# One more quartered pair in the up-projection, with one of the weights' sums made by an adding DMA

## The chip, the cores and the metric

One core of a Trainium2 chip runs the whole kernel. The metric is the device time of one execution in microseconds (us); of several runs the median counts. A profile of one further execution shows what each engine did: TensorE (PE, matmuls; its weight loads are PEld), VectorE (DVE), ScalarE (ACT), GpSimd (POOL), SyncE (SP, which here only issues DMAs) and the DMA engines.

## The reference

One decoder block on 512 tokens of width 1024, in float32: an attention sub-layer with two mixers, and a gated MLP with a short convolution. Only the second one's up-projection is touched:

```python
def conv_ffn(h, w_up, conv_w, conv_b, w_down):
    u = h @ w_up                       # (512, 1024) @ (1024, 2 * 2816)
    up = jnp.pad(u, ((0, 0), (CONV_WIDTH - 1, 0), (0, 0)))
    c = conv_b + conv_w[0] * up[:, 0:s]
    for j in range(1, CONV_WIDTH):
        c = c + conv_w[j] * up[:, j:j + s]
    val, gate = jnp.split(c, 2, axis=-1)
    return (jax.nn.silu(gate) * val) @ w_down
```

## The kernel before

Matmuls keep float32 accuracy by splitting each operand into a high part (rounded to the matmul's type, `whi`, made by ACT) and the low rest (`wlo`, made by DVE as raw − whi). A product is then three matmuls: high by high, high by low, low by high. `hh` and `hl` are the two parts of the normalized activations, features on the 128 partitions, tokens along the row.

The up-projection has 5632 output columns. They are worked off in 22 pairs: 128 gate columns and the 128 value columns that they will multiply. The list `order` says which columns come n-th; "pair 7" below is the pair at place 7 of `order`, counted from 0. A plain pair is two groups of 24 matmuls of 512 tokens (`dense_fm`), each into one PSUM bank. For places in `QUARTERED` the pair's product is computed in another way: the weights (1024 features by 256 columns) are cut in four quarters (upper or lower half of the features, gate or value columns: b11, b12 of the upper half, b21, b22 of the lower) and the tokens in halves. Sums of quarters by sums of the activations' quarters give the result with seven products in place of eight (Strassen's method in Winograd's form). Each product is 12 matmuls of 256 tokens, so a quartered pair is 84 matmuls of 256 in place of 48 of 512. The sums of the activations (`token_sums`) are made once, early; those of the weights for each pair, on DVE.

After each pair, `conv` takes gate and value out of PSUM (one ACT and two DVE instructions each, L129 and L141), Silu and the product with the value follow, and every second pair `sums` prepares sums and high and low parts for the down-projection, which uses the same trick.

The weights come through `wload`: SP issues a DMA into one of three places `raw` of 512 KB, which rotate. A plain pair needs two loads; a quartered pair two: "top" (upper half: b11 and b12) and "low" (b21, b22), each issued as two DMAs of 256 KB. Before, where the pair ahead was quartered too, "low" went to a fourth place, in the tile `right` (that was pair 8 alone). `first_quarters` makes what the first products need, ahead of the pair: the sums d, t1, t2 of the quarters, `h0`, `l0` (the parts of b11 and t1 for products −1 and 0) and `t3` (for product 2). `quartered` then makes `h1`, `l1` (t2 and b21) and `h2`, `l2` (the last ones) while PE is at the first products. Products 1 and 2 use the same bank `W` (tag `ps_a`), which ACT copies to `U` in `hB` between them.

Instructions are put in order per engine by a list scheduler when the program is built; each engine then works in that order and waits on semaphores.

The names in the rows: `ps_mm` and `ps_a` are the PSUM banks of results, `ps_b` a PSUM bank that here holds a weights' sum, `s` and `TS` the tiles with the activations' sums (and, in `s`, product 2's weights), `right` and `hB` the tiles in which pairs are finished. L1561 is the first matmul of a quartered pair, L126 the others, L123 those of plain pairs; L132 are tensor_tensor instructions of DVE, L323 the low parts of plain pairs' weights, L287 the loads of quartered pairs.

Of the kernel before, what the change touches and what calls it, by code (L numbers as in the profile page):

```python
# [16 lines left out]
ALU = mybir.AluOpType  # L17
# [7 lines left out]
KT = D // 128  # L25
# [58 lines left out]
def hybrid_block(ctx: ExitStack, tc: tile.TileContext, A: dict, out: bass.AP):  # L84
    nc = tc.nc
# [33 lines left out]
    def pb():  # L119
        return bank("b", 2)  # L120
# [10 lines left out]
    def tt(o, a, b, op):  # L131
        v.tensor_tensor(o, a, b, op=op)  # L132
# [7 lines left out]
    def stt(o, a, s, b, op0=ALU.mult, op1=ALU.add):  # L140
        v.scalar_tensor_tensor(o, a, s, b, op0=op0, op1=op1)  # L141
# [23 lines left out]
    for name in ("rwkv_mu", "rwkv_w0", "rwkv_a0", "rwkv_k_k", "rwkv_k_a", "rwkv_r_k", "rwkv_ln_g", "rwkv_ln_b"):  # L165
        r0, n = ROWS[name]
# [51 lines left out]
    hl = hp.tile([128, KT, S], F32R, name="hl", tag="hl")  # L218

    order = [f for i in range(NFH) for f in (i, NFH + i)]  # L220
    QUARTERED = (5, 7, 8, 10, 12, 14, 16, 18)

    def weight_tiles():
        def cols(w, o, kt=KT, eng=v):
            return w[:, o:o + 128], kt, 128, eng

        def rows(w, o, n, kt=KT, eng=v):
            step = 1024 // n
            for i, k0 in enumerate(range(0, kt, step)):
                kn = min(step, kt - k0)  # L230
                yield w[128 * k0:128 * (k0 + kn), o:o + n], kn, n, eng[i] if type(eng) is list else eng

        pool_ = nc.gpsimd
        yield cols(w_in, O_RWKV + 1536, eng=pool_)
        yield cols(w_in, O_RWKV + 1664, eng=pool_)
        for p in range(NH2):
            for o in (512, 0, 1024):
                yield cols(w_in, O_RWKV + o + 128 * p)
        yield cols(w_in, O_KC)
        yield from rows(w_in, O_Q, 512, eng=[v, pool_, ("spare", pool_), v])  # L240
        yield cols(w_in, O_VC)
        yield from rows(w_in, O_KS, 256, eng=[v, ("spare", v)])
        for m in range(NGA):
            yield cols(w_in, O_GA + 128 * m)
        yield from rows(w_in, O_KW, 280, eng=pool_)
        for m in range(NGA, KT):
            if m < 4:
                for s4 in range(m if m > NGA else 0, m + 1):
                    for s_ in "kv":
                        yield A["cmp_w1_" + s_][0][512 * s4:512 * s4 + 512], 4, 256, "ab" if (s4, s_) == (3, "k") else None  # L250
            yield cols(w_in, O_GA + 128 * m)
        for m in range(NGB):
            yield cols(w_in, O_GB + 128 * m)
        for m in range(KT):
            if m + NGB < KT:
                yield cols(w_in, O_GB + 128 * (m + NGB), eng=pool_ if m else v)
            yield cols(A["w_proj_b"][0], 128 * m, NH2, eng=pool_)
        for m in range(KT):
            yield cols(A["w_proj_a"][0], 128 * m, NH2)
        yield from rows(A["w_out"][0], 0, 512)  # L260
        yield from rows(A["w_out"][0], 512, 512, eng=())
        for n_, f in enumerate(order):
            if n_ in QUARTERED:
                for kh in range(2):
                    yield A["w_up"][0][512 * kh:512 * kh + 512], KT, 128, ("quarters", f, kh and n_ - 1 in QUARTERED)
            else:
                yield cols(A["w_up"][0], DFF + 128 * f)
                yield cols(A["w_up"][0], 128 * f)
# [3 lines left out]
    def wload():  # L272
        nxt = next(wtiles, None)
        if nxt is None:
            if spent:
                spent[0]()
        else:
            src, kt, n, eng = nxt
            if eng == "ab":
                raw, eng = AB[:, 0].rearrange("p a r t -> p (a r t)").rearrange("p (k n) -> p k n", n=n), None  # L280
            elif type(eng) is tuple and eng[:1] == ("quarters",) and eng[2]:
                raw = right[:, 6:8].rearrange("p a (k n) -> p (a k) n", n=n)
            else:
                raw = wp.tile([128, kt, n], F32, name="raw", tag=f"raw{next(slots) % 3}", bufs=1)
            if type(eng) is tuple and eng[:1] == ("quarters",):
                for i, c0 in enumerate((DFF + 128 * eng[1], 128 * eng[1])):
                    nc.sync.dma_start(raw[:, 4 * i:4 * i + 4], src[:, c0:c0 + 128].rearrange("(k p) n -> p k n", p=128))  # L287
                eng = "quarters"
            else:
                nc.sync.dma_start(raw, src.rearrange("(k p) n -> p k n", p=128))  # L290
            loads.append((raw, kt, n, eng))
# [64 lines left out]
    with tc.manual_schedule(engines={getattr(mybir.EngineType, e) for e in ("PE", "Activation", "DVE", "Pool")}):  # L356
# [3 lines left out]
        hi = wp.tile([128, KT, 128], F32R, name="whi", tag="whi", bufs=2)  # L360
        lo = wp.tile([128, KT, 128], F32R, name="wlo", tag="wlo", bufs=2)
        raw = loads.pop(0)[0]
# [21 lines left out]
        r0, n = ROWS["rwkv_mu"]  # L384
# [260 lines left out]
    for k in range(31):  # L645
        m, n = 31 - k, k + 1
# [845 lines left out]
    def token_sums():  # L1492
        for kh in range(2):
            def total(o, K, i):
                ks, ns = slice(4 * K + 2 * kh, 4 * K + 2 * kh + 2), slice(256 * i, 256 * i + 256)
                tt(o, hh[:, ks, ns].bitcast(F32), hl[:, ks, ns].bitcast(F32), ALU.add)

            x, y, z, w = [right[:, i].rearrange("p (k n) -> p k n", k=2) for i in range(3, 7)]
            total(x, 0, 1)
            total(y, 1, 1)  # L1500
            tt(y, x, y, ALU.add)
            yield
            total(z, 0, 0)
            tt(x, z, x, ALU.subtract)
            tt(z, y, z, ALU.subtract)
            yield
            total(w, 1, 0)
            tt(w, w, z, ALU.subtract)
            for j, o in enumerate((y, z, x, w)):
                hi, lo = sum_parts(j, kh)  # L1510
                act(hi, o)
                tt(lo, o, hi.bitcast(F32), ALU.subtract)
                if j % 2:
                    yield
# [9 lines left out]
    def halves(hi, lo, x):  # L1524
        act(hi, x)
        tt(lo, x, hi.bitcast(F32), ALU.subtract)
# [6 lines left out]
    def by_quarter(w):  # L1533
        return w.rearrange("p (q k) n -> p q k n", q=2)

    def first_quarters(top, low):
        b11, b12, b21, b22 = top[:, 0:4], top[:, 4:8], low[:, 0:4], low[:, 4:8]
        hi, lo = two_quarters()
        d = pb().rearrange("p (k n) -> p k n", k=4)
        tt(d, b22, b12, ALU.subtract)  # L1540
        tt(b12, b12, b11, ALU.subtract)
        halves(hi, lo, by_quarter(top))
        tt(b11, b22, b12, ALU.subtract)
        y = 2 * (next(turnsq) % 2)
        t3 = [split[y + j][:, :, NFH - 3].rearrange("p q (k n) -> p q k n", k=2) for j in range(2)]
        halves(*t3, by_quarter(d))
        return b11, low, (hi, lo), t3

    def quartered():
        t2, low, (h0, l0), (h3, l3) = ahead.pop(0)  # L1550
        b21 = low[:, 0:4]
        G, V, W = mmb(), mmb(), pa()[:, 0:256]
        act(V[:, 0:256], kc[:, 0:256], AF.Copy, scale=0.0)
        U = hB[:, 256 * (NFH + 3):256 * (NFH + 5)]

        def product(o, hi, lo, j, start=False):
            his, los = ([w[:, k] if len(w.shape) == 3 else w[:, k // 2, k % 2] for k in range(4)] for w in (hi, lo))
            for k in range(4):
                mh, ml = moving(j, k)
                if start and k == 0:  # L1560
                    te.matmul(o, lhsT=his[k], rhs=mh, start=True, stop=False, skip_group_check=True)  # L1561
                else:
                    mm_on(o, his[k], mh, False)
                mm_on(o, his[k], ml, False)
            for k in range(4):
                mm_on(o, los[k], moving(j, k)[0], False)

        wload()
        h1, l1 = two_quarters()
        halves(h1[:, 0], l1[:, 0], t2)  # L1570
        halves(h1[:, 1], l1[:, 1], b21)
        product(W, h0[:, 0], l0[:, 0], -1, True)
        act(G[:, 0:256], W)
        product(V[:, 0:256], h0[:, 1], l0[:, 1], 0)
        act(V[:, 256:512], V[:, 0:256])
        h2, l2 = two_quarters()
        tt(b21, b21, t2, ALU.subtract)
        halves(h2, l2, by_quarter(low))
        product(W, h1[:, 0], l1[:, 0], 1)
        act(U[:, 0:256], W)  # L1580
        product(G[:, 0:256], h1[:, 1], l1[:, 1], -2)
        wsplit()
        product(W, h3, l3, 2)
        act(G[:, 256:512], W)
        act(U[:, 256:512], W)
        product(V[:, 0:256], h2[:, 1], l2[:, 1], 3)
        product(G[:, 256:512], h2[:, 0], l2[:, 0], -3)
        tt(V, V, U, ALU.add)
        return G, V

    def sums(i, lf, rt):
# [257 lines left out]
```

## Time and profile before

| | |
|---|---|
| median of 3 runs | 806.47 us (805.72 to 807.74) |
| profiled execution | 805.58 us, its span 803.8 us |
| PE busy | 797.0 us (99%) |
| DVE busy | 634.9 us (79%) |
| ACT busy | 457.7 us (57%) |
| POOL busy | 64.7 us (8%) |
| first matmuls of the 8 quartered pairs | 515.4 to 652.1 us |
| granted TensorE clock | 0.999 of full speed |

The span runs from the first to the last instruction; the execution's own time has some overhead around it. A row of the timeline gives start, duration, engine, line, operation, out<-in with shapes, how many were merged, and in brackets how long the engine was idle before it and what ended that. A row of a windows table gives, for each engine, busy time and the number of instructions. The queues of SP and POOL are written SPq and POOLq where DMAs are issued.

### The profile page before, as it was taken

The numbers are of one execution on the slowest core, as the hardware profiler recorded it, in microseconds if no ns is written. First come the engines' busy times: TensorE is split into PE (matmuls) and PEld (weight loads), VectorE is DVE, ScalarE is ACT, GpSimd is POOL, SyncE is SP. The second block draws the span as 40 slices with busy tenths as digits, with TensorE's granted clock in tenths as the row PEclk, the third lists the DMA queues.
The fourth block names the chain that finished last, engine by engine and source line by source line (L and its number), as shares of the span: only waits on it lengthen the run. The fifth ranks groups of instructions, "written<-read, shape, count | busy, mean of one in ns | idle before, by whom it ended". The sixth has DMA issues, their size and how long they took to land.

```text
span 803.8 us, 14340 instructions
## 1 busy us (share of the span) xinstructions
PE 797.0 (99%) x5541; PEld 664.4 (83%) x5541; DVE 634.9 (79%) x1227; ACT 457.7 (57%) x931; POOL 64.7 (8%) x96
## 2 busy tenths in 40 slices
PE   8999999999999999999999999999999999999998
PEld 7777788987777887787788898899999998888886
DVE  6477869993665678889675589999999987898895
ACT  6766654563444568778334375666666665446452
POOL 6200011032000044011000000000000000000010
PEclk9999999999999999999999999999999999999999
DMA  8433213227562231001258322233233334376821
GB/s 240 115 79 79 79 54 105 70 81 208 143 117 68 70 83 50 15 27 32 63 177 283 103 83 82 83 108 115 86 103 106 105 106 129 120 235 220 276 95 52
DMA packets 114512, 89.30 MB, mean 111 GB/s; under 512 B 4886, under 2 KB 99021, under 8 KB 114189
## 3 DMA queue, kind: packets, MB, share of 16 engines
q1 hardware_dynamic: 110960, 82.83, 35.4%
q0 software_dynamic: 2432, 3.09, 1.5%
q10 hardware_dynamic: 1052, 2.48, 0.9%
q8 instruction: 43, 0.70, 0.4%
q14 instruction: 25, 0.20, 0.1%
HBM read 82.35 MB, written 4.39 MB: 108 GB/s over the span
## 4 chain that ended last, share of the span: by engine, by line
PE 94%; DVE 3%; ACT 1%; issue 0%; DMA 0%; DVEq 0%; ACTq 0%
PE ps_mm L123 62%; PE ps_mm L126 9%; PE ps_a L123 7%; PE ps_a L126 6%; PE ps_b L123 4%; PE ps_b L126 2%; PE ps_b L1304 1%; PE ps_mm L1304 1%; DVE P L1230 0%; DMA xt<-in_x_dram 0%; DVE P L136 0%; ACT P L129 0%; PE ps_b L591 0%; DVE wlo L132 0%; PE ps_b L560 0%
## 5 line engine op out<-in xcount | busy, mean ns | idle before, releaser
L123 PE MATMUL ps_mm<-hh,whi 128*128 128x512 f32 (+1 forms) x496 | 192.8, 391 | 0.3 <-DVE hl L141 0.3
L123 PE MATMUL ps_mm<-hl,whi 128*128 128x512 f32 (+1 forms) x496 | 190.6, 387 | 0.0
L129 ACT ACTIVATE whi<-raw 128x1024 fp32r<-128x1024 f32 (+2 forms) x132 | 124.5, 944 | 111.9 <-PE ps_mm L123 70.3
L123 PE MATMUL ps_mm<-hh,wlo 128*128 128x512 f32 (+1 forms) x496 | 120.4, 383 | 0.0
L323 DVE TENSOR_TENSOR wlo<-raw,whi 128x1024 fp32r<-128x1024 f32 (+1 forms) x73 | 84.7, 1162 | 41.7 <-PE ps_mm L123 21.6
L123 PEld LDWEIGHTS ps_mm<-hh,whi 128*128 128x128 f32 x496 | 93.2, 188 | 21.8 <-issue 1.3
L123 PEld LDWEIGHTS ps_mm<-hl,whi 128*128 128x128 f32 x496 | 93.3, 188 | 17.8 <-issue 1.0
L123 PEld LDWEIGHTS ps_mm<-hh,wlo 128*128 128x128 f32 x496 | 91.1, 188 | 18.5
L132 DVE TENSOR_TENSOR wlo<-raw,whi 128x1024 fp32r<-128x1024 f32 (+1 forms) x46 | 46.9, 1023 | 7.8 <-ACT whi L129 5.3
L141 DVE SCALAR_TENSOR_TENSOR right<-ps_mm,cw,right 128x511 f32<-128x511 f32 (+1 forms) x56 | 41.1, 743 | 4.4 <-ACT right L129 4.2
L129 ACT ACTIVATE P<-P,nm 128x512 f32<-128x512 f32 (+3 forms) x64 | 35.4, 554 | 11.4 <-DVE nm L1230 10.9
L323 POOL TENSOR_TENSOR wlo<-raw,whi 128x512 fp32r<-128x512 f32 (+3 forms) x13 | 20.9, 1605 | 177.0 <-PE ps_mm L123 142.6
L1746 POOL DMA_DIRECT2D out_dram<-XP x4 | 2.2, 549 | 391.3 <-DMA raw<-in_w_down_dram 389.7
L1230 DVE CUSTOM_DVE_ANT_0 P<-ps_a,AB 128x512 f32<-128x512 f32 (+3 forms) x64 | 29.3, 484 | 1.8 <-PE ps_a L123 1.5
L129 ACT ACTIVATE right<-ps_mm,cw 128x512 f32<-128x512 f32 x28 | 21.4, 772 | 9.9 <-DVE ps_mm L132 7.8
L129 ACT ACTIVATE QK<-ps_mm 128x64 f32<-128x64 f32 (+5 forms) x56 | 14.9, 308 | 18.0 <-PE ps_mm L123 17.9
L123 PE MATMUL ps_mm<-whi,hh 128*128 128x280 f32 (+2 forms) x72 | 22.4, 331 | 0.0
L123 PE MATMUL ps_mm<-whi,hl 128*128 128x280 f32 (+2 forms) x72 | 21.8, 323 | 0.0
L129 ACT ACTIVATE whi<-T 128x1024 fp32r<-128x1024 f32 (+1 forms) x12 | 11.9, 991 | 16.4 <-DVE T L132 7.5
L132 DVE TENSOR_TENSOR raw<-raw 128x512 f32<-128x512 f32 (+1 forms) x25 | 18.7, 747 | 2.7 <-DMA raw<-in_w_down_dram 2.7
L129 ACT ACTIVATE whi<-hA 128x1024 fp32r<-128x1024 f32 (+1 forms) x14 | 13.4, 969 | 12.8 <-PE ps_mm L126 3.7
L123 PE MATMUL ps_mm<-obT,whi 128*128 128x512 f32 x64 | 20.7, 399 | 0.0
(498 smaller groups left out, 1856.7 us busy)
## 6 DMA issues: line engine op xcount, KB each, us to landing
raw<-in_w_in_dram SPq DMA_DIRECT2D x38, 512.0 KB, 3.9
raw<-in_w_up_dram SPq DMA_DIRECT2D x28, 512.0 KB, 3.9
raw<-in_w_down_dram SPq DMA_DIRECT2D x18, 512.0 KB, 3.9
raw<-in_w_up_dram SPq DMA_DIRECT2D x30, 256.0 KB, 3.8
hA<-in_w_down_dram SPq DMA_DIRECT2D x12, 512.0 KB, 4.5
raw<-in_w_out_dram SPq DMA_DIRECT2D x8, 512.0 KB, 4.7
xt<-in_x_dram SPq DMA_DIRECT2D x4, 512.0 KB, 4.6
raw<-in_cmp_w_v_dram SPq DMA_DIRECT2D x4, 512.0 KB, 3.8
```

The lines of the kernel that those rows point to most:

```text
L123: te.matmul(o, lhsT=l, rhs=r, start=start, stop=stop)
L126: te.matmul(o, lhsT=l, rhs=r, start=False, stop=stop, skip_group_check=True)
L129: sc.activation(o, i, f, **kw)
L132: v.tensor_tensor(o, a, b, op=op)
L141: v.scalar_tensor_tensor(o, a, s, b, op0=op0, op1=op1)
L323: low = eng.tensor_tensor(lo, raw, hi.bitcast(F32), op=ALU.subtract)
L1230: maxima.append(v.tensor_tensor_reduce(out=P[:, i], in0=o, in1=BT[:, h, 384 - 128 * qt:512], scale=-1.0, scalar=-NEG, op0=ALU.add, op1=ALU ...
L1304: te.transpose(pt[:, 128 * i:128 * i + 128], P[:, 4 * x + i, 128 * k:128 * k + 128], ident)
L1746: queue.dma_start(out[0][128 * t:128 * t + 128, 512 * hf + cs.start:512 * hf + cs.stop], o)
```

## The change

Places 5, 7, 8, 10, 11, 13, 14, 16, 18 are quartered in place of 5, 7, 8, 10, 12, 14, 16, 18: nine pairs, and three times two in a row. The fourth raw place goes. The signs of some sums are moved from the weights to the activations, so that the first sum of the weights is an addition, b12 + b11, and that one is made by a DMA that adds: once "top" has landed, GpSimd issues a transfer from its one half to the other with `accum_op=add`. The value columns come out with the other sign, which the last combination takes back.

```diff
-    QUARTERED = (5, 7, 8, 10, 12, 14, 16, 18)
+    QUARTERED = (5, 7, 8, 10, 11, 13, 14, 16, 18)
...
-            elif type(eng) is tuple and eng[:1] == ("quarters",) and eng[2]:
-                raw = right[:, 6:8].rearrange("p a (k n) -> p (a k) n", n=n)
             else:
                 raw = wp.tile([128, kt, n], F32, name="raw", tag=f"raw{next(slots) % 3}", bufs=1)
             if type(eng) is tuple and eng[:1] == ("quarters",):
                 for i, c0 in enumerate((DFF + 128 * eng[1], 128 * eng[1])):
                     nc.sync.dma_start(raw[:, 4 * i:4 * i + 4], src[:, c0:c0 + 128].rearrange("(k p) n -> p k n", p=128))
+                if not eng[2]:
+                    nc.gpsimd.dma_start(raw[:, 4:8], raw[:, 0:4], accum_op=ALU.add)
...
     (token_sums)
-            tt(y, x, y, ALU.add)
+            tt(y, y, x, ALU.subtract)
...
-            tt(z, y, z, ALU.subtract)
+            stt(z, y, -1.0, z, ALU.mult, ALU.subtract)
...
-            tt(w, w, z, ALU.subtract)
+            stt(w, w, -1.0, z, ALU.mult, ALU.subtract)
...
     def first_quarters(top, low):
-        b11, b12, b21, b22 = top[:, 0:4], top[:, 4:8], low[:, 0:4], low[:, 4:8]
+        b11, t1, b22 = top[:, 0:4], top[:, 4:8], low[:, 4:8]
         hi, lo = two_quarters()
-        d = pb().rearrange("p (k n) -> p k n", k=4)
-        tt(d, b22, b12, ALU.subtract)
-        tt(b12, b12, b11, ALU.subtract)
         halves(hi, lo, by_quarter(top))
-        tt(b11, b22, b12, ALU.subtract)
+        t2 = pb().rearrange("p (k n) -> p k n", k=4)
+        tt(t2, b22, t1, ALU.add)
+        tt(b11, t2, b11, ALU.subtract)
...
-        halves(*t3, by_quarter(d))
-        return b11, low, (hi, lo), t3
+        halves(*t3, by_quarter(b11))
+        return t2, low, (hi, lo), t3
...
     (quartered)
-        tt(b21, b21, t2, ALU.subtract)
+        tt(b21, t2, b21, ALU.add)
...
-        tt(V, V, U, ALU.add)
+        stt(V, V, -1.0, U, ALU.mult, ALU.subtract)
```

How the instructions stand now. GpSimd's queue, from the attention part to the end of the program, after:

```order
L323 TENSOR_TENSOR wlo<-raw,whi 128x512 x7
L287 DMA raw<-raw 128x512 x9
L1745 DMA out_dram<-XP 128x512 x4
```

The nine adding transfers (L287 of the changed kernel) stand alone between the split of the attention part's last weights and the first stores.

SP's queue, the loads of pairs 5 to 15 (4 DMAs a quartered pair, 2 a plain one; `128x4x128` is a quarter, `128x8x128` half a plain pair), before and after:

```order
-L287 DMA raw<-in_w_up_dram 128x4x128 x4
-L287 DMA right<-in_w_up_dram 128x4x128
+L285 DMA raw<-in_w_up_dram 128x4x128 x4
 L290 DMA raw<-in_w_up_dram 128x8x128 x2
-L287 DMA raw<-in_w_up_dram 128x4x128 x6
+L285 DMA raw<-in_w_up_dram 128x4x128 x8
 L290 DMA raw<-in_w_up_dram 128x8x128 x2
-L287 DMA raw<-in_w_up_dram 128x4x128 x4
+L285 DMA raw<-in_w_up_dram 128x4x128 x8
 L290 DMA raw<-in_w_up_dram 128x8x128 x2
```

The loads into `right` are gone, and eight quarters stand in a row where two quartered pairs do.

DVE, the preparation of pair 7 while PE is at pair 6 (`ps_b<-raw` is the pair's first sum on DVE, d before and t2 after; `wlo` of 128x1024 is `l0`):

```order
 L132 TENSOR_TENSOR ps_b<-raw 128x512
 L141 SCALAR_TENSOR_TENSOR right<-ps_mm,cw,right 128x510
-L132 TENSOR_TENSOR raw<-raw 128x512
-L132 TENSOR_TENSOR s_5189<-ps_b,s_5188 128x2x256
+L132 TENSOR_TENSOR wlo<-raw,whi 128x1024
 L132 TENSOR_TENSOR right<-hB,right 128x512
 L141 SCALAR_TENSOR_TENSOR right<-ps_mm,cw,right 128x511
```

The sum on DVE is gone, product 2's part has moved back, and `l0` has moved to the front.

PE in pair 8, from the second half of product 1 (`ps_a<-TS,whi`) to the start of product 2 (`ps_a<-s_5188,s_5186`). Before:

```order
L126 MATMUL ps_a<-TS,whi 128x256 x4
L126 MATMUL ps_mm<-hh_4674,whi 128x256
L126 MATMUL ps_mm<-hl_4675,whi 128x256
L126 MATMUL ps_mm<-hh_4674,whi 128x256
L126 MATMUL ps_mm<-hl_4675,whi 128x256
L126 MATMUL ps_mm<-hh_4674,whi 128x256
L126 MATMUL ps_mm<-hl_4675,whi 128x256
L126 MATMUL ps_mm<-hh_4674,whi 128x256
L126 MATMUL ps_mm<-hl_4675,whi 128x256
L126 MATMUL ps_mm<-hh_4674,wlo 128x256 x3
L126 MATMUL ps_a<-s_5187,wlo 128x256 x2
L126 MATMUL ps_a<-TS,wlo 128x256 x2
L126 MATMUL ps_mm<-hh_4674,wlo 128x256
L126 MATMUL ps_a<-s_5188,s_5186 128x256 x4
```

After, the same pair:

```order
L126 MATMUL ps_a<-TS,whi 128x256 x4
L126 MATMUL ps_a<-s_5187,wlo 128x256 x2
L126 MATMUL ps_a<-TS,wlo 128x256 x2
L126 MATMUL ps_mm<-hh_4674,whi 128x256
L126 MATMUL ps_mm<-hl_4675,whi 128x256
L126 MATMUL ps_mm<-hh_4674,whi 128x256
L126 MATMUL ps_mm<-hl_4675,whi 128x256
L126 MATMUL ps_mm<-hh_4674,whi 128x256
L126 MATMUL ps_mm<-hl_4675,whi 128x256
L126 MATMUL ps_mm<-hh_4674,whi 128x256
L126 MATMUL ps_mm<-hl_4675,whi 128x256
L126 MATMUL ps_mm<-hh_4674,wlo 128x256 x4
L126 MATMUL ps_a<-s_5188,s_5186 128x256 x4
```

Product 1's low half (`ps_a<-s_5187,wlo`) stood in the midst of another product, one matmul ahead of product 2; now twelve matmuls stand between. In pair 14 of the changed kernel it stands so:

```order
L126 MATMUL ps_a<-s_5187,wlo 128x256 x2
L126 MATMUL ps_a<-TS,wlo 128x256 x2
L126 MATMUL ps_mm<-hh_4674,whi 128x256
L126 MATMUL ps_mm<-hl_4675,whi 128x256
L126 MATMUL ps_a<-s_5188,s_5186 128x256 x3
L126 MATMUL ps_mm<-hh_4674,wlo 128x256 x4
L126 MATMUL ps_a<-s_5188,s_5186 128x256
```

There two matmuls stand between product 1's end and product 2. In the other quartered pairs of the changed kernel it is twelve.

More of the change, by code (lines that the diff above doesn't have):

```diff
@@ L264, in weight_tiles @@
                 for kh in range(2):
-                    yield A["w_up"][0][512 * kh:512 * kh + 512], KT, 128, ("quarters", f, kh and n_ - 1 in QUARTERED)
+                    yield A["w_up"][0][512 * kh:512 * kh + 512], KT, 128, ("quarters", f, kh)
             else:
```

## The prediction

> **What bounds the kernel now.** I read the page's head and its chain of work first, then the busy times in stretches of the up-projection, then single rows there.
>
> ```profile
> span 803.8 us, 14340 instructions
> PE 797.0 (99%) x5541; PEld 664.4 (83%) x5541; DVE 634.9 (79%) x1227; ACT 457.7 (57%) x931; POOL 64.7 (8%) x96
> PE 94%; DVE 3%; ACT 1%; issue 0%; DMA 0%; DVEq 0%; ACTq 0%
> ```
>
> TensorE (PE) is busy for 99% of the span and carries 94% of the chain. A change moves the time only by removing matmul time or by making PE wait. The changed part runs from 515.4 us (the first quartered pair) to 662. The windows below are, in this order, pairs 7, 8, 9 together (two quartered, one plain), then twice one quartered and one plain pair (10 and 11; 12 and 13).
>
> ```profile
> core 0: us, PE busy (x) PEld busy (x) DVE busy (x) ACT busy (x) POOL busy (x), PEclk, DMA share, GB/s
> 536.50:568.17 31.67, 31.31 (x218) 29.21 (x216) 30.46 (x48) 20.99 (x39) 0.00 (x0) 1.00 0.29 84
> 568.17:589.15 20.98, 20.98 (x134) 19.08 (x132) 19.30 (x31) 13.12 (x24) 0.00 (x0) 1.00 0.35 101
> 589.15:610.13 20.98, 20.98 (x134) 19.09 (x132) 19.14 (x30) 12.84 (x25) 0.00 (x0) 1.00 0.35 101
> ```
>
> The granted clock is 1.00 throughout, GpSimd (POOL) is idle, the DMA engines are a third busy, and VectorE (DVE) is the second engine: 91% in the alternating stretch and 96% where two quartered pairs stand together (30.46 of 31.67).
>
> Prices of the two kinds of pair: a plain group of 24 matmuls, and a quartered pair from its first matmul (L1561) to the next pair's.
>
> ```profile
> 477.34 0.39 PE L123 MATMUL ps_mm<-hh,whi 128*128 128x512 f32 x1
> 482.78 0.39 PE L123 MATMUL ps_mm<-hh,whi 128*128 128x512 f32 x1
> ...
> 536.50 0.28 PE L1561 MATMUL ps_a<-hh,whi 128*128 128x256 f32 x1
> 546.57 0.28 PE L1561 MATMUL ps_a<-hh,whi 128*128 128x256 f32 x1
> ```
>
> A plain group takes 482.78 − 477.34 = 5.44 us, so a plain pair 10.88. A quartered pair takes 546.57 − 536.50 = 10.07; from the alternating window it is 20.98 − 10.88 = 10.10.
>
> **The change, part by part.**
>
> *The ninth quartered pair.* One plain pair becomes a quartered one: 48 matmuls of 512 columns leave, 84 of 256 come. 10.88 − 10.08 = 0.80 us less on PE, and PE is the bound. The ninth pair brings its own work beside it, on ACT and DVE (below).
>
> *The stall in pair 8.* The whole up-projection has one wait of PE:
>
> ```profile
> PE ps_a L126 <- ACT hB L129: 0.4, 1, 0.4
> ...
> 552.21 0.28 PE L126 MATMUL ps_mm<-hh,wlo 128*128 128x256 f32 x1
> 552.84 0.39 PE L126 MATMUL ps_a<-s,s 128*128 128x256 f32 x1 [0.36 <-ACT hB L129]
> ...
> 552.41 0.38 ACT L129 ACTIVATE hB<-ps_a 128x256 f32<-128x256 f32 x1 [1.86 <-PE ps_a L126]
> ```
>
> Product 2 reuses the bank of product 1, which ACT must first copy out (552.41, 0.38). One matmul of 0.12 us stands between them, because the order of before put product 1's low half behind the K half of another product. From 552.21 to 552.84 is 0.63 where 0.12 would do: 0.5 us lost (the window's 31.67 against 20.98 + 10.08 = 31.06 says 0.6; I take 0.6). The new order of pair 8 has twelve matmuls there, so this goes: −0.6. The same interleaving now stands in pair 14, with two matmuls between: 0.5 − 0.12, so +0.4.
>
> *VectorE.* Two stretches' difference prices a quartered pair on DVE: 30.46 − 19.2 = 11.3 us, a plain one 19.2 − 11.3 = 7.9.
>
> ```profile
> L132 DVE TENSOR_TENSOR raw<-raw 128x512 f32<-128x512 f32 x20 | 13.6, 682 | 0.0
> L132 DVE TENSOR_TENSOR ps_b<-raw 128x512 f32<-128x512 f32 x6 | 4.1, 689 | 0.0
> L323 DVE TENSOR_TENSOR wlo<-raw,whi 128x1024 fp32r<-128x1024 f32 x12 | 14.6, 1218 | 0.9 <-ACT whi L129 0.9
> 529.21 0.69 DVE L132 TENSOR_TENSOR ps_b<-raw 128x512 f32<-128x512 f32 x1
> 529.80 0.74 DVE L141 SCALAR_TENSOR_TENSOR right<-ps_mm,cw,right 128x510 f32<-128x510 f32 x1
> ...
> 534.92 1.22 DVE L132 TENSOR_TENSOR wlo<-raw,whi 128x1024 fp32r<-128x1024 f32 x1
> ```
>
> Of three sums (682 and 689 ns, starting 0.59 apart) one leaves DVE per pair: 10.7 us. Reading t2 from PSUM instead of SBUF, and the sums that become scalar_tensor_tensor (0.74 against 0.69), are 0.05 each: nothing. Two quartered pairs and a plain one then need 2 × 10.7 + 7.9 = 29.3 of PE's 31.06 us (94%; before 96%), but such groups come three times in a row, pairs 7 to 15, where before there was one. One and one need 18.6 of 20.98. Spare: 1.8 and 2.4 us per group. ACT does as many instructions per quartered pair as before (21 of 31.7 us busy): covered.
>
> *The waits that move with it.* The first pieces now come from the high half: h0's low part stood at 534.92, 5.7 us after the pair's first sum; in the new order it is the second instruction after it. t2, and what hangs on it, is needed on PE only at the second and third product (12 and 24 matmuls of 0.12, 1.4 and 2.9 us later). So the late load, low's, has more time than before. No fourth place: the top place is free once t2 is in PSUM, so low of 8, 11, 14 can go there; their loads start when the pair before has its first pieces (for pair 7 534.92 + 1.22 = 536.1, 10 us before pair 8's first matmul), against 3.8 us to land (next fence). Covered.
>
> *The adding transfer.* Per pair POOL issues one transfer of 256 KB that adds b11 to b12 on chip. The trace has none that adds. Nearest rows: on-chip transfers of the POOL queue (KH), and its 256 KB stores.
>
> ```profile
> L1073 POOL DMA_DIRECT2D KH<-KH x4: 509/512/576, 279.1 to 285.6; - x4
> DMA to landing us min/median/max: 2.2/2.5/3.9
> out_dram<-XP POOLq DMA_DIRECT2D x4, 256.0 KB, 2.8
> ...
> raw<-in_w_up_dram SPq DMA_DIRECT2D x30, 256.0 KB, 3.8
> 522.09 0.92 SPq L287 DMA_DIRECT2D raw<-in_w_up_dram  x2
> 552.33 0.92 SPq L287 DMA_DIRECT2D raw<-in_w_up_dram  x2
> 574.57 0.98 SPq L287 DMA_DIRECT2D raw<-in_w_up_dram  x2
> ...
> 562.07 0.69 DVE L132 TENSOR_TENSOR ps_b<-raw 128x512 f32<-128x512 f32 x1
> 581.86 0.69 DVE L132 TENSOR_TENSOR ps_b<-raw 128x512 f32<-128x512 f32 x1
> ```
>
> Bounds of issue to landing: 2.2 us (the fastest on-chip one), and 7.8 (the slowest, 3.9, twice, since an addition also reads its target). I take 3.5: the store of the same size, 2.8, and a quarter more. Issuing it costs POOL 0.51 us, and POOL has nothing else there: behind its waits queue only the next adding transfers and, 100 us later, the stores. Is it in time? On DVE the sum t2 waits for it, and all evictions queue behind t2. Pair 7: the second top load starts at about 522.5, lands 3.8 later at 526.3, the sum lands at 529.8; t2's turn is at 529.2. Pair 10: 552.8 + 3.8 + 3.5 = 560.1 against 562.07. Pairs like 12 of before (now 16, 18): 575.05 + 3.8 + 3.5 = 582.35 against 581.86. So DVE waits about half a microsecond at three pairs, under its spare 1.8 to 2.4: nothing on PE. Pairs 8, 11, 14 have their top loaded a pair ahead: covered. Below zero this edit can't go on PE beyond the 0.6 already counted, since PE waits nowhere else.
>
> The row: POOL issues took 0.51 us at 279 us beside a working DVE. [...]
>
> **The sum.** −0.8 − 0.6 + 0.4 = −1.0 us. The profiled execution took 805.58 us (span 803.8 and 1.8 around it), 0.9 below the runs' median of 806.47. The runs spread over 2.0 us, so about 0.3% (2.4 us) is what can be told from no change. For the median: 806.47 − 1.0 = 805.5.
>
> **Rivals.**
>
> A. *DVE becomes the bound in the second of two quartered pairs.* For it: the only stall of before sits in such a pair, with DVE at 96%. Against: one sum less per pair, and the alternating stretch shows no stall at 91%. If 8, 11 and 14 each lose 0.6, it is 1.8 in place of 0.4: 806.9.
>
> B. *The adding transfer is late; slower than before.* With L its time to landing, DVE stands idle for L − 2.9 at pair 7, L − 3.0 at 16 and 18, L − 5.5 at 10 and 13 (from the landings above), less the spare 1.8, 2.4 and 1.8. [...] At 7.8 it is 3.1 + 2 × 2.4 + 2 × 0.5 = 8.9: 814.4. It is slower by over 0.3% from L = 6.3 on (3L − 15.5 = 3.4). For it: no row shows an addition. Against: all POOL rows are at 3.9 or less, and an addition would have to double the slowest.
>
> C. *Pair 14 doesn't stall* since DVE is less loaded than the order's maker assumed: 805.1.
>
> D. *The ninth pair's gain doesn't show.* Half of it could be lost where the extra start-up of a pair is not hidden; then 805.9, not told from the forecast.
>
> **How the numbers follow.** Forecast with D 0.62, A 0.18, B 0.11 (two thirds of it beyond L = 6.3), C 0.07, something unseen 0.02. The largest gain, 0.8 + 0.6 = 1.4, is 0.17%, so faster by over 0.3% needs a lucky median: 0.03. Slower: 0.07 from B, 0.03 from A worse than priced or unseen: 0.10. Same: 0.87. Range: from C less half the runs' spread, 805.1 − 1.0 = 804.1, to A plus the same, with the lower part of B: 808.2.
>
> **What would show it.** Right: nine first matmuls of quartered pairs, the pairs' distances 10.07 to 10.10 (7 to 8, 10 to 11, 13 to 14), 20.98 for one and one, the wait on ACT hB gone in pair 8 and, at about 0.4, in pair 14; adding transfers landing in 2.2 to 5 us. Wrong: PE waits for whi or wlo at a second quartered pair (A), DVE idle before ps_b<-raw with the transfer as releaser (B), or a pair 18 that begins later than 652.1 − 1.0 = 651.1 with no wait listed.

## The result: nine pairs take 9.4 us longer, and the profile after

| | before | after |
|---|---|---|
| median | 806.29 us (805.72 to 807.74) | 815.71 us (814.96 to 816.13, 4 runs) |
| profiled execution | 805.58 us, span 803.8 us | 814.96 us, span 813.2 us |

The ratio is 1.0113, with an interval of 1.0096 to 1.0131. The change is slower by 1.1%, where no measurable change was forecast. In the table, before has one run more than in the table ahead of the prediction. One of the ten executions of the second experiment below took 2773 us, for a reason that no record shows, and its ratio leaves it out.

The page of after, its head:

```profile
span 813.2 us, 14455 instructions
PE 799.1 (98%) x5577; PEld 666.2 (82%) x5577; DVE 634.0 (78%) x1226; ACT 460.2 (57%) x940; POOL 73.1 (9%) x105
```

No engine has become the bound: DVE is busy no longer than before (634.0 against 634.9), yet the span is 9.4 us longer. PE's busy time has grown by 2 us, although 0.8 us of matmuls left, and that too comes from waits: a matmul of 256 tokens is recorded with 0.28 us where the next follows after 0.12 (569.80, then 569.92), so the first 0.16 of a wait counts as busy, and in the trace the one behind a wait is followed after 0.22. In the up-projection PE stood idle at 12 places, four of them for at most 0.11 us and not in the list below; these 0.26 at each make 3.1 us beside the waits that are listed. The busy times in stretches of after, cut at the first matmuls of pairs 5, 7, 10, 13, 16 and 18:

```profile
core 0: us, PE busy (x) PEld busy (x) DVE busy (x) ACT busy (x) POOL busy (x), PEclk, DMA share, GB/s
516.05:537.03 20.98, 20.98 (x133) 19.09 (x132) 17.55 (x28) 12.33 (x23) 1.74 (x2) 1.00 0.50 126
537.03:569.33 32.30, 31.92 (x218) 29.41 (x216) 27.16 (x44) 19.63 (x37) 1.72 (x2) 1.00 0.43 115
569.33:603.68 34.35, 31.82 (x217) 29.31 (x216) 30.03 (x48) 20.87 (x39) 1.73 (x2) 1.00 0.39 105
603.68:638.53 34.85, 32.35 (x217) 29.46 (x216) 29.38 (x49) 21.03 (x40) 0.87 (x1) 1.00 0.37 102
638.53:661.67 23.14, 21.49 (x134) 19.19 (x132) 21.36 (x34) 14.49 (x27) 0.87 (x1) 1.00 0.38 103
```

The first stretch takes exactly one quartered and one plain pair's 20.98. Each of the three groups of two quartered pairs and a plain one should take 20.98 + 10.08 = 31.06; they take 32.30, 34.35 and 34.85. The last should take 20.98 and takes 23.14. Lost: 1.24 + 3.29 + 3.79 + 2.16 = 10.5 us. Before lost 0.7 on this way (136.67 from 515.42 to 652.09, against 6 × 20.98 + 10.08 = 135.96). So from pair 5 to pair 18 it is 10.5 − 0.7 − 0.8 (the ninth pair) = +9.0. Pair 5 starts 0.6 later, and the rest after pair 18 takes 0.2 less: 9.4 in all.

Who waits, by the waits of after from 500 to 670 us (engine, tile and line; for what; total, times, longest):

```profile
ACT whi L129 <- DMA raw<-raw: 19.7, 5, 5.7
DVE ps_b L132 <- DMA raw<-raw: 10.6, 5, 3.7
PE ps_a L126 <- ACT ps_mm L129: 5.6, 5, 1.8
PE ps_a L126 <- DVE wlo L132: 0.8, 1, 0.8
PE ps_a L126 <- ACT hB L129: 0.4, 2, 0.2
```

`raw<-raw` is the adding transfer. It holds up not only DVE, as the prediction had it, but ACT twice as long. PE never waits for the transfer itself; it waits for what stands behind it, five times in ACT's queue and once in DVE's (`wlo`, 0.8). Pair 10 shows how, in rows of the timeline of after (SP and POOL, then ACT, DVE, PE):

```profile
556.37 0.92 SPq L285 DMA_DIRECT2D raw<-in_w_up_dram  x2
562.04 0.86 POOL L287 DMA_DIRECT2D raw<-raw  x1 [27.45 <-DVE right L141]
...
559.33 1.43 ACT L129 ACTIVATE right<-ps_mm,cw 128x512 f32<-128x512 f32 x2
566.46 1.06 ACT L129 ACTIVATE whi<-raw 128x1024 fp32r<-128x1024 f32 x1 [5.70 <-DMA raw<-raw]
...
573.70 0.38 ACT L129 ACTIVATE ps_mm<-ps_a 128x256 f32<-128x256 f32 x1
...
566.32 0.70 DVE L132 TENSOR_TENSOR ps_b<-raw 128x512 f32<-128x512 f32 x1 [3.01 <-DMA raw<-raw]
...
571.96 0.40 PE L126 MATMUL ps_mm<-TS,wlo 128*128 128x256 f32 x2
574.13 0.74 PE L126 MATMUL ps_a<-s,whi 128*128 128x256 f32 x4 [1.77 <-ACT ps_mm L129]
```

Top's two loads are issued at 556.37; before they went out at 552.33. The second lands at 561.4, POOL issues the transfer at 562.04, and the sum is there at 566.3, 9.9 us after the load's issue. ACT's next instruction, the high part of top (`whi<-raw`), needs the sum and stands idle for 5.70 us; behind it queue Silu, evictions and the copy `ps_mm<-ps_a` at 573.70, which takes product −1 out of the bank where product 1 goes. PE has run dry at 572.4 and waits for that copy. ACT is not alone in it: between 566.46 and 573.70 it waits twice more, 0.43 and 0.84 us, for DVE, whose own queue began late with the sum t2 at 566.32.

The median transfer is what was forecast (view of its line), but the three that hurt most are slower:

```profile
L287 POOL DMA_DIRECT2D raw<-raw x9: 862/865/937, 505.5 to 651.4; - x9
DMA to landing us min/median/max: 3.2/3.6/6.2
...
629.78 0.87 POOL L287 DMA_DIRECT2D raw<-raw  x1 [27.41 <-DVE wlo L323]
635.99 0.70 DVE L132 TENSOR_TENSOR ps_b<-raw 128x512 f32<-128x512 f32 x1 [3.69 <-DMA raw<-raw]
```

By the landings in the trace those of pairs 8, 11 and 14, with no load under way beside them, took 3.2 to 3.3 us; those of pairs 10, 13 and 16, issued amid loads, took 4.3, 4.7 and 6.2 (the rows above are pair 16's). Not every transfer beside loads was slow, though: pair 18's took 3.7.

### The profile page after: what moved, and what is told of

Same layout as the page of the kernel before. It is cut to its first block, busy times and chain, and to the rows that moved or that the text cites. A ratio compares the mean times of both kernels' runs of the same rounds, so it can differ in the third digit from the quotient of the medians.

```text
span 813.2 us, 14455 instructions
## 1 busy us (share of the span) xinstructions
PE 799.1 (98%) x5577; PEld 666.2 (82%) x5577; DVE 634.0 (78%) x1226; ACT 460.2 (57%) x940; POOL 73.1 (9%) x105
## 5 line engine op out<-in xcount | busy, mean ns | idle before, releaser
L129 ACT ACTIVATE whi<-raw 128x1024 fp32r<-128x1024 f32 (+3 forms) x127 | 121.6, 961 | 132.5 <-PE ps_mm L123 66.2
L123 PE MATMUL ps_mm<-hh,whi 128*128 128x512 f32 (+1 forms) x480 | 186.5, 391 | 0.3 <-DVE hl L141 0.3
L123 PE MATMUL ps_mm<-hl,whi 128*128 128x512 f32 (+1 forms) x480 | 184.3, 387 | 0.0
L123 PE MATMUL ps_mm<-hh,wlo 128*128 128x512 f32 (+1 forms) x480 | 116.5, 382 | 0.0
L323 DVE TENSOR_TENSOR wlo<-raw,whi 128x1024 fp32r<-128x1024 f32 (+1 forms) x71 | 82.4, 1162 | 43.5 <-ACT whi L129 22.7
L123 PEld LDWEIGHTS ps_mm<-hh,whi 128*128 128x128 f32 x480 | 90.2, 188 | 21.2 <-issue 1.3
L123 PEld LDWEIGHTS ps_mm<-hl,whi 128*128 128x128 f32 x480 | 90.3, 188 | 17.2 <-issue 1.0
L123 PEld LDWEIGHTS ps_mm<-hh,wlo 128*128 128x128 f32 x480 | 88.1, 188 | 17.8
L132 DVE TENSOR_TENSOR wlo<-raw,whi 128x1024 fp32r<-128x1024 f32 (+1 forms) x43 | 46.4, 1084 | 7.3 <-ACT whi L129 6.8
L287 POOL DMA_DIRECT2D raw<-raw x9 | 7.9, 874 | 263.5 <-DMA raw<-in_w_up_dram 158.5
L129 ACT ACTIVATE s<-hB 128x256 fp32r<-128x256 f32 x33 | 13.3, 409 | 10.4 <-DVE hB L132 10.2
```

The source lines that it names most:

```text
L123: te.matmul(o, lhsT=l, rhs=r, start=start, stop=stop)
L129: sc.activation(o, i, f, **kw)
L287: nc.gpsimd.dma_start(raw[:, 4:8], raw[:, 0:4], accum_op=ALU.add)
L323: low = eng.tensor_tensor(lo, raw, hi.bitcast(F32), op=ALU.subtract)
```

## The experiments

Three theories. W: ACT and DVE wait in order for the adding transfer, which comes late. F: the missing fourth place makes the next pair's top load late, since "low" of the second quartered pair keeps the place that it needs. A: as rival A of the prediction, VectorE is full where two quartered pairs stand together, whoever makes the sums. "The change" below is the kernel after; n is a pair's place. Each ratio is to before, on the same chip; medians of different kernels can come from different chips. The diffs are shortened: where the condition keeps a transfer from being issued, `first_quarters` begins with `tt(t1, t1, b11, ALU.add)`, VectorE's sum.

**VectorE makes all nine sums, no transfer.**

```diff
-                    nc.gpsimd.dma_start(raw[:, 4:8], raw[:, 0:4], accum_op=ALU.add)
...
+            tt(t1, t1, b11, ALU.add)   # in first_quarters
```

> The changed kernel with all nine first sums (b12 + b11) made by VectorE again, as its first instruction of a pair's preparation, and no adding transfer; nine pairs, same places, no fourth raw place. Theory W (the way from load over transfer to sum is longer than the time ahead of a pair, so ScalarE and VectorE stand before it with all else queued behind): the 9 us go away, 805 to 808. Theory A (VectorE is the bound where two quartered pairs follow each other): nothing goes away or it gets worse, since VectorE has 0.6 us more per pair: 815 to 818. Theory F (without the fourth place the loads come too late, whoever adds): most of the loss stays, 811 to 815.

Measured: 808.18 us, ratio 1.0022 (1.0013 to 1.0031). 7.5 us of the loss are gone with the transfer, so W holds, if just above its range; some 2 us remain against before, so it isn't all.

**A transfer only in the second pair of two (n = 8, 11, 14); VectorE in the others.**

```diff
-                if not eng[2]:
+                if not eng[2] and n - 1 in QUARTERED:
                     nc.gpsimd.dma_start(raw[:, 4:8], raw[:, 0:4], accum_op=ALU.add)
```

> The changed kernel with the adding transfer only for pairs 8, 11 and 14, whose upper weights are loaded a pair ahead; VectorE makes the sum for 5, 7, 10, 13, 16, 18. Theory W: no transfer is waited for, and VectorE is relieved where it is fullest: 804.5 to 807, at or below the kernel with all sums on VectorE. Theory A: 813 to 816. Theory F: 811 to 815.

Measured: 807.75 us, ratio 1.0019 (1.0009 to 1.0029). That too is above W's range. The three transfers whose top is loaded a pair ahead cost nothing against the first experiment; the harm of the change sits in the other six, and not in all of these, as the next run shows.

**Before's eight places, all sums by transfer, no fourth place.**

```diff
-    QUARTERED = (5, 7, 8, 10, 11, 13, 14, 16, 18)
+    QUARTERED = (5, 7, 8, 10, 12, 14, 16, 18)
```

> The changed kernel with the eight places of before (5, 7, 8, 10, 12, 14, 16, 18): all sums by transfer, no fourth raw place, only pairs 7 and 8 adjacent. Theory W: the waits stay where loads are late, at pair 10 (behind two adjacent ones, some 2 us) and by 0 to 1 us at 12 to 18: 807 to 811. Theory A: without the adjacent pairs the loss is gone: 805.5 to 807. Theory F: only pair 10 is late: 807 to 809, with the wait there on the load and not on the transfer.

Measured: 809.40 us, ratio 1.0038 (1.0026 to 1.0050). Its waits:

```profile
ACT whi L129 <- DMA raw<-raw: 10.9, 3, 5.5
PE ps_a L126 <- ACT ps_mm L129: 1.5, 1, 1.5
```

From pair 12 on each quartered and plain pair takes 20.98: transfers at 12, 14 and 16 cost nothing. Pair 10, the one whose top waits for the place of a second pair's "low", takes 23.05 with its plain pair, and there sits PE's wait of 1.5 (pairs 7 and 8 lose 1.3 together). So it isn't the transfer as such (W alone) but the transfer behind a late load (F and W).

**A plain copy in place of the adding transfer** (b12 is overwritten, the sum is left out).

```diff
-                    nc.gpsimd.dma_start(raw[:, 4:8], raw[:, 0:4], accum_op=ALU.add)
+                    nc.gpsimd.dma_start(raw[:, 4:8], raw[:, 0:4])
```

> The changed kernel with the transfer as a plain copy of b11 over b12 in place of an addition (the first sum is left out, so the result is another one): same bytes, same waits. Theory W: the addition costs nothing of its own, landing stays at 3 to 4 us and the time at 813 to 816. Rival: reading the target and adding is what makes the transfer late; the copy lands in 2 to 2.8 us and the time falls to 805 to 811.

Measured, one execution: 811.73 us. The copy's line, and ACT's wait for it:

```profile
L287 POOL DMA_DIRECT2D raw<-raw x9: 548/548/572, 505.4 to 648.2; - x9
DMA to landing us min/median/max: 2.2/2.3/5.0
  ACT whi L129: 11.7, 3
```

A copy lands 1.3 us sooner than an addition (2.3 against 3.6) and is issued 0.3 us faster, and that gives back 4.0 of the 9.4 us; the time lies between the two expected ranges. The rest stays: with these places and late loads a copy is too late as well.

**Eight places, VectorE makes all sums, no fourth place.** The first experiment's edit with before's places.

```diff
-    QUARTERED = (5, 7, 8, 10, 11, 13, 14, 16, 18)
+    QUARTERED = (5, 7, 8, 10, 12, 14, 16, 18)
...
-                    nc.gpsimd.dma_start(raw[:, 4:8], raw[:, 0:4], accum_op=ALU.add)
...
+            tt(t1, t1, b11, ALU.add)   # in first_quarters
```

> Eight places as before, all first sums on VectorE, no fourth raw place, the new signs: of the change only the missing place and the signs are left. Theory F (the missing place alone makes the loads behind two adjacent pairs late and costs time): 807 to 808, with pair 10 late. Theory A (VectorE too full where three times two pairs adjoin is what remains beside the transfer): as before or 0.6 less, 805.3 to 806.5, since only pairs 7 and 8 adjoin.

Measured: 807.02 us, ratio 1.0012 (1.0003 to 1.0022). F's number came, but not where F has it. Pair 10's top is again issued late, yet nothing waits for it. DVE's one wait for a load stands elsewhere, ahead of pair 12:

```profile
556.61 0.92 SPq L285 DMA_DIRECT2D raw<-in_w_up_dram  x2
...
582.54 0.70 DVE L132 TENSOR_TENSOR ps_b<-raw 128x512 f32<-128x512 f32 x1 [1.78 <-DMA raw<-in_w_up_dram]
...
PE ps_a L126 <- ACT hB L129: 0.5, 1, 0.5
```

It costs nothing: from pair 10 to 18 each quartered and plain pair takes 20.98. Nearly all of the loss from pair to pair is in pairs 8 and 9, which take 22.12 where before took 21.60 (31.67 − 10.07), with PE's wait in pair 8. The kernel with VectorE's sums and the fourth place (below) takes the same 22.12 there, with the same wait, so this is the sum on VectorE and not the place. The other 0.7 us of the profiled execution are a later start of pair 5 (516.16). So without any transfer the missing place is not shown to cost anything here.

**The change with the fourth place, for "low" of 8 and 11.**

```diff
+            elif type(eng) is tuple and eng[:1] == ("quarters",) and eng[2] and n in (8, 11):
+                raw = right[:, 6:8].rearrange("p a (k n) -> p (a k) n", n=n)
```

> The changed kernel (nine pairs, all sums by transfer) with the fourth raw place again for low of 8 and 11, so that the loads of 10 and 13 need not wait for it. If the late start of these loads is a part of the transfer's lateness (theory W with F in it): ScalarE's wait for the transfer shrinks by some 4 us at 10 and at 13, and the time falls by 2 to 5 us, to 811 to 814. If the transfer is late whatever the loads do (W alone): 815 to 816.

Measured: 809.50 us, ratio 1.0037 (1.0024 to 1.0050), 6.2 us below the change. Pair 10 in its timeline, PE's waits from 500 to 670 us, and where DVE (pair 7) and ACT (pair 16) still wait for a transfer:

```profile
548.29 0.92 SPq L287 DMA_DIRECT2D raw<-in_w_up_dram  x2
552.81 0.86 POOL L289 DMA_DIRECT2D raw<-raw  x1 [18.14 <-DVE right L132]
...
PE ps_a L126 <- ACT ps_mm L129: 1.6, 1, 1.6
PE ps_a L126 <- ACT hB L129: 0.5, 2, 0.4
...
531.58 0.70 DVE L132 TENSOR_TENSOR ps_b<-raw 128x512 f32<-128x512 f32 x1 [1.80 <-DMA raw<-raw]
629.04 1.06 ACT L129 ACTIVATE whi<-raw 128x1024 fp32r<-128x1024 f32 x1 [5.52 <-DMA raw<-raw]
```

Top is loaded 8 us sooner, the sum is there at 556.1 in place of 566.3, and the groups from 10 and 13 take 31.25 and 32.04 in place of 34.35 and 34.85. What is left: pair 7, where DVE waits 1.80 and the pair takes 10.83, and pair 16, where ACT waits 5.52 and the pair with its plain one takes 23.13; it follows "low" of 14, which has no fourth place here, and costs PE its 1.6 again.

**Eight places, fourth place, a transfer for pair 8 alone.** This is before, but with the signs moved and one sum on chip.

```diff
-    QUARTERED = (5, 7, 8, 10, 11, 13, 14, 16, 18)
+    QUARTERED = (5, 7, 8, 10, 12, 14, 16, 18)
...
+            elif type(eng) is tuple and eng[:1] == ("quarters",) and eng[2] and n in (8, 11):   # 11 is plain here
+                raw = right[:, 6:8].rearrange("p a (k n) -> p (a k) n", n=n)
...
-                if not eng[2]:
+                if not eng[2] and n - 1 in QUARTERED:   # else the sum in first_quarters
```

> Eight places as before, fourth raw place as before, the adding transfer for pair 8 alone, new signs: the parts of the change that cost nothing by W, A and F. All three: 805.3 to 806.3, the stall of 0.6 us in pair 8 gone or not; if it is slower than that, the signs or the transfer's traffic cost something that no theory has.

Measured: 805.90 us, ratio 0.9999 (0.9990 to 1.0008). In its trace PE waits nowhere in the up-projection (pairs 8 and 9 take 21.05), so pair 8's stall is gone and the new signs cost nothing. But its first quartered pair starts at 515.91, 0.5 later than before, and the total doesn't show the gain.

**Nine places from 4 on**, with two double pairs in place of three; sums as in the second experiment.

```diff
-    QUARTERED = (5, 7, 8, 10, 11, 13, 14, 16, 18)
+    QUARTERED = (4, 6, 8, 9, 11, 13, 14, 16, 18)
```

> Nine pairs at 4, 6, 8, 9, 11, 13, 14, 16, 18 (two adjacent groups in place of three), transfers for 9 and 14 alone, VectorE's sums for the others, no fourth place. Theory A: the loss per adjacent group (about 1 us of the 1.7 above before) falls by a third, 805.5 to 807, unless VectorE is too full at pairs 4 to 6, beside the activations' sums. Theory F: two groups in place of three, 806.5 to 807.5.

Measured: 812.35 us, ratio 1.0075 (1.0059 to 1.0091). It fails at a new place: at pair 4 VectorE still makes the activations' sums (`s`) and is busy without a gap (4.86 of 4.86 in this window's DVE column), while PE waits for a low part.

```profile
509.00:513.86 4.86, 1.04 (x9) 0.83 (x7) 4.86 (x13) 1.17 (x3) 0.00 (x0) 1.00 0.32 93
...
513.86 0.51 PE L126 MATMUL ps_a<-s,wlo 128*128 128x256 f32 x2 [3.83 <-DVE wlo L132]
```

**VectorE makes all nine sums, with the fourth place for 8 and 11**, the edits of the first experiment and of the sixth.

```diff
+            elif type(eng) is tuple and eng[:1] == ("quarters",) and eng[2] and n in (8, 11):
+                raw = right[:, 6:8].rearrange("p a (k n) -> p (a k) n", n=n)
...
-                    nc.gpsimd.dma_start(raw[:, 4:8], raw[:, 0:4], accum_op=ALU.add)
...
+            tt(t1, t1, b11, ALU.add)   # in first_quarters
```

> Nine pairs at the places of the change, all first sums on VectorE, fourth raw place for low of 8 and 11: neither the transfer nor (but for pair 16) the late loads, only the three adjacent groups are left. Theory A: still 1.5 us or more above before, 807 to 808. If the missing place is what made the kernel with VectorE's sums slow: 805 to 806.5, some 2 us below it.

Measured: 807.65 us, ratio 1.0022 (1.0013 to 1.0031). The first experiment's ratio is the same, so the place is worth nothing that can be told here (0.3 us of medians, each against before on its chip), and not the 2 that were missing. Its stretches of pairs 7, 10 and 13:

```profile
538.10:570.30 32.20, 31.69 (x218) 29.34 (x216) 30.96 (x50) 21.84 (x42) 0.00 (x0) 1.00 0.34 99
570.30:602.41 32.11, 31.61 (x217) 29.27 (x216) 30.53 (x50) 20.31 (x38) 0.00 (x0) 1.00 0.29 83
602.41:634.30 31.89, 31.70 (x217) 29.32 (x216) 29.97 (x49) 21.39 (x41) 0.00 (x0) 1.00 0.34 99
```

Each takes 0.8 to 1.1 over 31.06, 3.0 together, with DVE busy for 94% to 96%. That is what theory A says. How it comes about stands in pair 8:

```profile
552.13 0.69 DVE L132 TENSOR_TENSOR wlo<-ps_b,whi 128x512 fp32r<-128x512 f32 x1
...
553.31 0.40 PE L126 MATMUL ps_a<-TS,wlo 128*128 128x256 f32 x2
554.18 0.62 PE L126 MATMUL ps_a<-s,s 128*128 128x256 f32 x3 [0.47 <-ACT hB L129]
```

DVE makes product 1's low part only at 552.13, so product 1's low half stands last and product 2 right behind it, with no matmul between to cover ACT's copy.

**The same with transfers for 8, 11 and 14**, the edits of the second experiment and of the sixth.

```diff
+            elif type(eng) is tuple and eng[:1] == ("quarters",) and eng[2] and n in (8, 11):
+                raw = right[:, 6:8].rearrange("p a (k n) -> p (a k) n", n=n)
...
-                if not eng[2]:
+                if not eng[2] and n - 1 in QUARTERED:   # else the sum in first_quarters
```

> The same with the transfer for 8, 11 and 14 in place of VectorE's sums there: VectorE has 0.6 us less in each adjacent group. Theory A: better than all sums on VectorE by 0.5 to 1.5 us, 805 to 807. Without A: the same as that kernel within 0.5.

Measured: 805.83 us, ratio 0.9996 (0.9987 to 1.0006). The same stretches:

```profile
539.05:570.18 31.13, 31.13 (x217) 29.23 (x216) 30.46 (x49) 21.83 (x42) 0.88 (x1) 1.00 0.40 111
570.18:601.40 31.22, 31.22 (x218) 29.27 (x216) 29.64 (x49) 20.18 (x38) 0.86 (x1) 1.00 0.34 94
601.40:633.37 31.97, 31.61 (x218) 29.31 (x217) 29.93 (x48) 21.74 (x41) 0.00 (x0) 1.00 0.34 99
```

With the second pair's sum off DVE the first two groups fall from 32.20 and 32.11 to 31.13 and 31.22, and the medians differ by 1.8 us. In pair 8 the low part of product 1 is made 0.55 us after the pair's first matmul here, 3.95 in the kernel above, and twelve matmuls stand between products 1 and 2. This shows A for the sums by VectorE, and that it ends with the transfer in the second pairs. DVE's share is no measure of it (30.46 of 31.13 is 98%, and next to nothing is lost), so it is the place of these instructions in the queues that counts; another order with the same work on DVE was not tried. Nor do the gains add: against before on the same chip the place alone brought 0.3 and the three transfers alone (second experiment) 0.4, neither clear of the noise, and both together 2.1. The 0.9 left in the third group is mostly PE's wait for `hB` in pair 14.

**Fourth place, transfers for all pairs but 7 and 16**, the two where the run with the fourth place and all transfers still waited.

```diff
-                if not eng[2]:
+                if not eng[2] and n not in (7, 16):   # with the fourth place as above
```

> Fourth place for low of 8 and 11, all sums by transfer but for pairs 7 and 16, whose transfers came late with the place (by VectorE there). Theory W with F: the waits of 0.75 us at 7 and 2.1 us at 16 of the kernel with the place and all transfers go away, 806 to 807; if a transfer costs also where it is in time, it stays at 808 or above.

Measured: 805.42 us (804.80 to 806.08), ratio 0.9991 (0.9982 to 1.0000). Stretches of pairs 7, 10, 13 and 16, and the only wait of PE:

```profile
536.84:567.90 31.06, 31.06 (x217) 29.17 (x216) 30.07 (x48) 21.69 (x41) 1.72 (x2) 1.00 0.47 123
567.90:599.12 31.22, 31.22 (x218) 29.27 (x216) 29.04 (x48) 20.19 (x38) 1.72 (x2) 1.00 0.39 102
599.12:631.02 31.90, 31.54 (x217) 29.26 (x216) 29.97 (x48) 21.73 (x41) 0.00 (x0) 1.00 0.34 99
631.02:652.00 20.98, 20.98 (x133) 19.09 (x132) 18.74 (x29) 13.38 (x24) 0.86 (x1) 1.00 0.42 114
...
PE ps_a L126 <- ACT hB L129: 0.4, 1, 0.4
```

Two transfers fewer than in the run with the fourth place, and 4.1 us less (3.7 by the ratios). Its median is the lowest of all kernels, 0.4 us below before's on the same chip, at the edge of what can be told.

## Why the prediction was wrong, step by step

- **"No fourth place … Covered" failed, and together with the next step this is most of the loss.** It looked at whether "low" of 8, 11 and 14 arrives in time, and that it does. It didn't ask who gets the place after it: the top of 10, 13 and 16. That place is given up only when the last reader of "low" in a second quartered pair is through, so the load is issued at 556.37, not at the 552.33 that the next step took over from before. Giving the place back (for 8 and 11) brings 6.2 us while all sums are made by transfer; where VectorE makes them all it brings nothing clear, and 1.9 where transfers serve 8, 11 and 14 alone. So most of what the place cost came of the late load with a transfer behind it.
- **"The adding transfer … Is it in time?" failed.** Its guess of 3.5 us to landing was right for the median (3.6) and short at pairs 10, 13 and 16 (4.3, 4.7, 6.2); rival B's sign came, DVE idle before `ps_b<-raw`, but B as drawn, with L from 6.3 on, did not. What failed is the sum around it. For pair 10 it was to be there at 560.1 and came at 566.3. Of these 6.2 us, 4.0 are the late issue; 0.8 the load, which took 4.6 us in a burst of six rather than 3.8; 0.6 the time from its landing to POOL's issue, which the sum put at nothing; 0.8 the transfer itself. At pair 7, whose load waits for no second pair's "low", DVE waits 1.8 us in the run with the fourth place, where 0.6 was worked out: the load goes out 1.1 later than before, and POOL issues 0.8 after it has landed.
- **The same step priced the wait on one engine's queue only.** It compared with t2's turn on DVE, gave DVE a spare of 1.8 to 2.4 us, and took none of it to PE. `whi<-raw` reads the sum too, in ACT's queue, with the copies behind it that free PE's banks. The prediction called ACT covered by its busy time (21 of 31.7 us). It is only 57% busy, but its order is fixed: idle times of 5.70 us there and 3.01 on DVE became 1.77 on PE.
- **The +0.4 in pair 14 was mis-sized.** The wait on `hB` came as drawn, 0.4, but it costs more than its row shows (0.16 ahead of it and 0.10 behind), 0.6 in all; in the last run the group from 13 loses 0.8.
- **Right:** the pairs at 10.07 and 20.98 where nothing waits, pair 8's stall gone, signs at no cost, and VectorE's load: A shows when VectorE makes the second pairs' sums as well, not where those are made on chip. The last run is what the sum −1.0 looks like with its waits taken away: from pair 5 to 18 it takes 136.14 us against 136.67, so −0.5; the whole is −0.4 by the medians.

The 0.51 us for an issue was short too: POOL's issues of the nine adding transfers took 862 to 937 ns, with DVE busy for 6.90 of the 7.85 us that they make together. While the slowest transfer (pair 16, 6.2 us) was under way, DVE stood idle for 3.69 us. The range's upper end, 808.2, takes in rival B below L = 6.3; no run shows a landing near that as the common one: in the change the median was 3.6, and one of nine took 6.2.

Two things stay open. The first quartered pair at place 5 starts between 515.4 and 516.9 us from kernel to kernel (0.6 us of the 9.4 here), and at 517.9 in the profiled execution with transfers for 8, 11 and 14 and the place, whose mean granted clock was 0.997 (1.000 in the kernel after); what in the part ahead sets it is open. And whether ACT's high part of top, set later in its queue, would have spared PE the wait was not tried.

## What to carry to other kernels

When a buffer is taken away, ask not only whether the tile that moves is in time but who is next in the place it moves to, and when its last reader lets it go. When a wait is added, list every engine that reads the result, and follow each queue behind that reader down to the busiest engine: here the wait went through ACT, which looked idle, and through DVE. Measure a chain of load, transfer and reader from the load's issue to the reader's start in a crowded place, not as the sum of the median landings: at pair 10 it took 9.9 us, where the medians (3.4 for a load of 256 KB, 3.6 for the transfer) make 7.0.

## What the runs showed of the hardware

A transfer of 256 KB within the chip that adds took 3.6 us to landing in the median, against 2.3 for a plain copy of the same tiles, and POOL 0.86 us to issue against 0.55. With no load under way the adding ones landed in 3.2 to 3.3 us; among loads one took 6.2 (pair 16 of the change), and the slowest copy 5.0.

Behind one wait of PE the granted clock was lower. After the 3.83 us at pair 4 in the kernel with places from 4 on, the column behind POOL's shows 0.62, then 0.97:

```profile
513.90:518.00 4.10, 4.10 (x21) 4.03 (x22) 2.90 (x4) 2.39 (x3) 0.00 (x0) 0.62 0.00 0
518.00:522.00 4.00, 4.00 (x30) 3.82 (x29) 2.10 (x4) 2.21 (x4) 0.00 (x0) 0.97 0.77 221
```

Four matmuls of 256 columns in a row took 0.92 us there (from 514.46 on) and 0.64 in the kernel after (570.76); with 0.28 for the last one, they stood 213 ns apart and 120. A clock of 0.62 over 4.10 us lacks 0.38 of it, which makes about 1.6 us lost on top of the wait, by this estimate. After the waits of up to 1.8 us in the kernel after, the clock stayed at 1.00 (windows above).
